# A hybrid decoder layer in fp32 on one core: SwiGLU up-projections by one level of Strassen's algorithm, and a separate down phase

## The chip, the core and the metric

The kernel runs on one core of one Trainium2 chip. The metric is the device time of one execution in microseconds (us); lower is better. TensorE (PE) does matrix products and writes to the accumulators (PSUM), VectorE (DVE), ScalarE (ACT) and GpSimd (POOL) do elementwise work, SyncE (SP) issues the DMAs.

## The reference

One layer: half a SwiGLU feed-forward, a mixing block (sliding-window attention with sinks beside an S5 state-space scan, both gated), and another half feed-forward, over 1024 prompt tokens and 32 sample tokens (1056 columns in the kernel).

```python
D_MODEL = 1024; D_FF = 2816            # 22 tiles of 128

def rms_norm(x, g):
    return x * lax.rsqrt(jnp.mean(x * x, axis=-1, keepdims=True) + 1e-6) * g

def swiglu(x, w1, w3, w2):
    return (jax.nn.silu(x @ w1) * (x @ w3)) @ w2

def trunk_layer(x, ...):
    x = x + 0.5 * swiglu(rms_norm(x, ffn1_norm), ffn1_w1, ffn1_w3, ffn1_w2)
    ...                                  # h = rms_norm(x, mix_norm); proj = h @ w_in; attention; S5
    x = x + merged @ w_out
    x = x + 0.5 * swiglu(rms_norm(x, ffn2_norm), ffn2_w1, ffn2_w3, ffn2_w2)
```

## The kernel before

Features lie on the partitions (8 tiles of 128 for the model width), tokens on the columns: `T` = 1056 in `NC` = 3 chunks of `C` = 352. Every fp32 operand of a large product is split in a high and a low part of 12 bits each (`fp32r`), and a product is three passes: high x high, high x low, low x high (`gemm`, line 153). Weights come from DRAM in units of 8 blocks of 128x128 (`load_w`, line 142): one DMA, a ScalarE copy for the high part, a VectorE subtraction for the low one.

A feed-forward (`ffn`, line 242) goes through 11 groups of two tiles of the inner width. `g1` makes a tile's two up-products (`pa`, `pb`) for the three chunks from x times the norm's weight; `swi` (line 234) multiplies by 1/rms on the result, applies Silu, multiplies and splits. `g2` (line 213) adds the group before, times the rows of `w2`, to x; all inner activations stay in SBUF. The last group runs chunk by chunk, so that `run_last` (line 226) can split x for the next block and sum its squares (`xg_part`, `rstd`) behind it. 1/rms is thus needed only after a product, and the next products start on x itself.

At the start (`first`, line 454), x arrives in pieces of one chunk of one tile, and the first products follow each piece. `hook` (line 442) puts the parameters of the S5 scan beside feed-forward 1: one step of `params_b` in each group from the third on, mostly on GpSimd, with a few TensorE transposes. After the mixing, `merge` makes two tiles of the merged activations at a time, and `g2` adds the group before, times `w_out`, to x.

The order of instructions on each engine comes from the framework's planner, which simulates the program as it is built (`schedule_with_timeline_sim=True`); buffers come from pools with a fixed number of slots: accumulators `mm` and `sm` of four banks each, large tiles `X` (16), `T` (17) and `R` (2).

Of the kernel before, what the change touches and what calls it, by code (L numbers as in the profile page):

```python
# [21 lines left out]
KD = 8  # L22
# [3 lines left out]
NGS = 6         # gate tiles next to the SSM  # L26
# [10 lines left out]
def body(tc, I, O):  # L37
# [4 lines left out]
    with es:  # L42
# [4 lines left out]
        Xp = pool("X", 16)  # L47
        Tp = pool("T", 17)
        Rp = pool("R", 2)
        wr_p = pool("wr", 3)  # L50
        wl_p = pool("wl", 3)
        wh_p = pool("wh", 3)
        gt_p = pool("gt", 3)
        st_p = pool("st", 4)
        sq_p = pool("sq", 4)
        pp_p = pool("pp", 4)
        mm_p = pool("mm", 4, space=PSUM)
        sm_p = pool("sm", 4, space=PSUM)
        dr = pool("dr", 1, space=DRAM)

# [27 lines left out]
        def XT(name, dt=F32R):  # L88
            return big(Xp, "X", name, dt)
# [4 lines left out]
        def RT(name):  # L94
            return big(Rp, "R", name)

        def SQ(name):
            return sq_p.tile([128, C], F32, tag="sq", name=name)
# [4 lines left out]
        def MM(name):  # L103
            return mm_p.tile([128, 512], F32, tag="mm", name=name)[:, :C]

        def SM(name):
            return sm_p.tile([128, 512], F32, tag="sm", name=name)
# [3 lines left out]

        f32 = lambda a: a.bitcast(F32)

# [4 lines left out]
        one = SQ("one")[:, 0:128]  # L118
# [6 lines left out]
        onesh = cst.tile([128, 128], F32R, name="onesh")     # ones where both are of one head  # L125
# [10 lines left out]
        # the tensor engine's clock rises with use: work until the first operands are there  # L136
# [5 lines left out]
        def load_w(src, parts=1, copy=S.copy, lo=V):  # L142
            r = wr_p.tile([128, 8, 128], F32, tag="wr", name="wr")
            l = wl_p.tile([128, 8, 128], F32R, tag="wl", name="wl")
            h = wh_p.tile([128, 8, 128], F32R, tag="wh", name="wh")
            for i in range(parts):
                s = slice(8 // parts * i, 8 // parts * (i + 1))
                dma(r[:, s, :], src[:, s, :])
                copy(h[:, s, :], r[:, s, :])  # L149
                sub(l[:, s, :], r[:, s, :], f32(h[:, s, :]), lo)  # L150
            return h, l

        def gemm(name, c, wks, xs, sm=False):
            """one chunk of one tile of a product: sum over k of w_k^T x_k without the product of the low parts"""
            ps = SM(name)[:, :C] if sm else MM(name)
            n = len(wks)
            for k, (((h, l), kb), (xh, xl)) in enumerate(zip(wks, xs)):
                for i, (w, x) in enumerate(((h, xh), (h, xl), (l, xh))):
                    PE.matmul(ps, w[:, kb, :], x[:, cs(c)], start=k == 0 and i == 0, stop=k == n - 1 and i == 2)  # L159
            return ps  # L160
# [13 lines left out]
        def xg_split(x, g0, xs, k, c):  # L174
            h, l = xs[k]
            g = vec[:, g0 + k:g0 + k + 1]
            act(h[:, cs(c)], x[k][:, cs(c)], AF.Copy, scale=g)
            stt(l[:, cs(c)], x[k][:, cs(c)], g, f32(h[:, cs(c)]), ALU.mult, ALU.subtract)

        def xg_part(x, g0, xs, k, c, acc):  # L180
            xg_split(x, g0, xs, k, c)
            return xg_sq(x, k, c, acc)

        def xg_sq(x, k, c, acc, on_pool=False):
            s = SQ("sq")
            xc = x[k][:, cs(c)]
            if on_pool:
                mul(s, xc, xc, Pl)
            else:
                act(s, xc, AF.Square)  # L190
            if acc is not None:
                add(s, s, acc, Pl)
            return s

        def rstd(r, acc, c):
            ps = SM("ss")
            h, l = (sq_p.tile([128, C], F32R, tag="sq", name="acc" + n) for n in "hl")
            S.copy(h, acc)
            sub(l, acc, f32(h), Pl)
            for i, a in enumerate((h, l)):  # L200
                PE.matmul(ps[:, :C], ones, a, start=i == 0, stop=i == 1)
            y, a = SQ("y"), SQ("a")
            act(y, ps[:, :C], AF.Abs_reciprocal_sqrt, scale=1.0 / 1024, bias=epsx)
            mul(a, y, y)
            stt(a, ps[:, :C], 1024 * EPS, a, ALU.add, ALU.mult)
            ts(a, a, -0.5 / 1024, 1.5, ALU.mult, ALU.add)
            mul(r[:, cs(c)], y, a)
# [3 lines left out]

# [1 line left out]
        def g2(w2, g, hs, x, scale, last):  # L213
            wu = [load_w(w2[2 * g + j]) for j in range(2)]
            order = [(c, m) for c in range(NC) for m in range(KD)] if last else [(c, m) for m in range(KD) for c in range(NC)]
            for c, m in order:
                p = gemm("p2", c, blocks(wu[m // 4], (m % 4 * 2, m % 4 * 2 + 1)), hs)
                o = x[m][:, cs(c)]
                if scale is None:
                    add(o, p, o)  # L220
                else:
                    stt(o, p, scale, o, ALU.mult, ALU.add)
                if last:
                    yield c, m
# [9 lines left out]
        def swi(t, h, l, r, c, pa, pb):  # L234
            tc_ = t[:, cs(c)]
            mul(tc_, pa, r[:, cs(c)])
            act(tc_, tc_, AF.Silu)
            mul(tc_, tc_, r[:, cs(c)])
            mul(tc_, pb(), tc_)
            split(h, l, t, c)  # L240

        def ffn(w1, w3, w2, x, xs, r, hook=None, first=None):
            hs = {}
            ng = NFF // 2

            def g1(g):
                for f in (2 * g, 2 * g + 1):
                    if first and f == 0:
                        hs[f] = first()
                        continue  # L250
                    wa, wb = load_w(w1[f]), load_w(w3[f])
                    t = TT("t")
                    h, l = TT("hh", F32R), TT("hl", F32R)
                    for c in range(NC):
                        swi(t, h, l, r, c, gemm("pa", c, blocks(wa), xs), lambda: gemm("pb", c, blocks(wb), xs))
                    hs[f] = (h, l)

            g1(0)
            for g in range(1, ng):
# [875 lines left out]
```

## Time and profile before

| | us |
|---|---|
| median of 3 runs | 2180.45 (2179.9 to 2182.01) |
| span of the profiled execution | 2178.1 |
| TensorE busy in it | 2156.0 (13545 matmuls) |
| VectorE busy | 1238.8 |
| ScalarE busy | 633.5 |
| GpSimd busy | 390.2 |

The span runs from the first to the last instruction; the remainder of a run lies around it. Busy time of TensorE counts overlapping matmuls, so the distance between their starts tells more than their duration. Feed-forward 1 is the stretch up to about 800 us, the mixing lies between 800 and 1410 us, feed-forward 2 behind that.

### The profile page before, as it was taken

To read this page: it belongs to the slowest core of one execution; us is meant where nothing else is said; L and a number is where in the kernel's file an instruction comes from. 1 tells how busy PE (TensorE), PEld (TensorE's weight loads), DVE (VectorE), ACT (ScalarE), POOL (GpSimd) and SP (SyncE) were. 2 spreads that over 40 slices of the span, in tenths; PEclk is the share of its full clock that TensorE was granted. 3 is DMA by queue.
4 is the path that set the end of the run, shared out by engine and by line. 5 is a ranking of instruction groups with operands and counts; after the bars stand their busy time and mean duration, and the time that the engine had idled before them with its cause. 6 is when DMAs were issued, how large, how long until landed. Compare 5 with 4: busy or idle time off the path is not lost.

```text
span 2178.1 us, 33755 instructions
## 1 busy us (share of the span) xinstructions
PE 2156.0 (99%) x13545; PEld 2132.8 (98%) x13545; DVE 1238.8 (57%) x2357; ACT 633.5 (29%) x1223; POOL 390.2 (18%) x821
## 2 busy tenths in 40 slices
PE   9999999999999999999999999999999999999999
PEld 8999999999999999999998999999999999999999
DVE  9544444454444485758989966854444443444445
ACT  6322222222221152235456631441111111111110
POOL 5342234323430042425101100210000000000000
PEclk9999999999999999999999999999999999999999
DMA  5122112122111135632323571111111111111112
GB/s 184 40 77 63 61 55 72 63 61 65 58 61 59 40 119 197 204 96 75 99 81 114 191 287 47 40 49 49 49 39 41 57 42 45 50 40 49 49 40 80
DMA packets 83133, 173.55 MB, mean 80 GB/s; under 512 B 21200, under 2 KB 46096, under 8 KB 82960
## 3 DMA queue, kind: packets, MB, share of 16 engines
q1 hardware_dynamic: 82976, 171.39, 24.3%
q8 instruction: 106, 1.74, 0.3%
q14 instruction: 51, 0.42, 0.1%
HBM read 132.54 MB, written 35.95 MB: 77 GB/s over the span
## 4 chain that ended last, share of the span: by engine, by line
PE 90%; DVE 5%; ACT 1%; issue 1%; POOL 1%; DMA 1%; SPq 0%; DVEq 0%; ACTq 0%; POOLq 0%
PE p L159 26%; PE pb L159 22%; PE pa L159 22%; PE pj L159 11%; PE pm L159 4%; DVE xl L74 1%; PE pg L159 1%; POOL sq L62 1%; PE sc L766 1%; PE po L807 1%; DVE raw L62 1%; PE pt L792 1%; DVE wl L62 0%; DMA qw<-raw 0%; PE pv L564 0%
## 5 line engine op out<-in xcount | busy, mean ns | idle before, releaser
L74 DVE SCALAR_TENSOR_TENSOR x<-p,x 128x352 f32<-128x352 f32 x528 | 270.2, 522 | 164.8 <-PE p L159 164.2
L149 ACT CAST wh<-wr 128x1024 fp32r<-128x1024 f32 (+1 forms) x176 | 183.9, 1045 | 554.0 <-issue 202.3
L159 PE MATMUL pa<-xh,wh 128*128 128x352 f32 x1056 | 343.6, 325 | 1.4 <-DVE x L62 0.6
L159 PE MATMUL pa<-xl,wh 128*128 128x352 f32 x1056 | 342.3, 324 | 1.7 <-DVE xl L74 1.7
L159 PE MATMUL p<-hh,wh 128*128 128x352 f32 x1056 | 343.2, 325 | 0.3 <-DVE x L74 0.2
L159 PE MATMUL pb<-xh,wh 128*128 128x352 f32 x1056 | 342.4, 324 | 0.0
L159 PE MATMUL pa<-xh,wl 128*128 128x352 f32 x1056 | 342.3, 324 | 0.0
L159 PE MATMUL pb<-xh,wl 128*128 128x352 f32 x1056 | 341.1, 323 | 0.0
L159 PE MATMUL p<-hh,wl 128*128 128x352 f32 x1056 | 340.7, 323 | 0.0
L159 PE MATMUL pb<-xl,wh 128*128 128x352 f32 x1056 | 340.2, 322 | 0.0
L159 PE MATMUL p<-hl,wh 128*128 128x352 f32 x1056 | 340.2, 322 | 0.0
L62 DVE TENSOR_TENSOR wl<-wr,wh 128x1024 fp32r<-128x1024 f32 (+1 forms) x176 | 224.8, 1278 | 70.0 <-ACT wh L149 67.1
L159 PEld LDWEIGHTS pa<-xl,wh 128*128 128x128 f32 x1056 | 199.7, 189 | 4.0 <-DVE xl L74 4.0
L62 DVE TENSOR_TENSOR t<-pa,r 128x352 f32<-128x352 f32 x132 | 69.1, 524 | 233.7 <-PE pa L159 233.5
L159 PEld LDWEIGHTS p<-hh,wh 128*128 128x128 f32 x1056 | 198.5, 188 | 3.5 <-DVE x L74 1.8
L159 PEld LDWEIGHTS pa<-xh,wh 128*128 128x128 f32 x1056 | 199.2, 189 | 2.4 <-DVE x L62 0.9
L62 DVE TENSOR_TENSOR t<-pb,t 128x352 f32<-128x352 f32 x132 | 69.1, 524 | 230.0 <-PE pb L159 229.6
L159 PEld LDWEIGHTS pa<-xh,wl 128*128 128x128 f32 x1056 | 199.5, 189 | 0.2 <-DVE wl L62 0.2
L159 PEld LDWEIGHTS pb<-xl,wh 128*128 128x128 f32 x1056 | 199.1, 189 | 0.0
L159 PEld LDWEIGHTS p<-hl,wh 128*128 128x128 f32 x1056 | 198.8, 188 | 0.0
L159 PEld LDWEIGHTS pb<-xh,wl 128*128 128x128 f32 x1056 | 198.7, 188 | 0.0
L159 PEld LDWEIGHTS p<-hh,wl 128*128 128x128 f32 x1056 | 198.6, 188 | 0.0
(715 smaller groups left out, 3654.1 us busy)
## 6 DMA issues: line engine op xcount, KB each, us to landing
wr<-in_w_in SPq DMA_DIRECT2D x26, 512.0 KB
wr<-in_w2a SPq DMA_DIRECT2D x22, 512.0 KB
wr<-in_w1b SPq DMA_DIRECT2D x22, 512.0 KB
wr<-in_w3b SPq DMA_DIRECT2D x22, 512.0 KB
wr<-in_w2b SPq DMA_DIRECT2D x22, 512.0 KB
wr<-in_w1a SPq DMA_DIRECT2D x21, 512.0 KB
wr<-in_w3a SPq DMA_DIRECT2D x21, 512.0 KB
gd<-gt SPq DMA_DIRECT2D x48, 176.0 KB
```

The lines of the kernel that those rows point to most:

```text
L62: e.tensor_tensor(out=o, in0=a, in1=b, op=op)
L74: V.scalar_tensor_tensor(out=o, in0=a, scalar=s, in1=b, op0=op0, op1=op1)
L149: copy(h[:, s, :], r[:, s, :])
L159: PE.matmul(ps, w[:, kb, :], x[:, cs(c)], start=k == 0 and i == 0, stop=k == n - 1 and i == 2)
L766: PE.matmul(o, st[e_][:, q0:q0 + 128], kk[:, k0:k0 + nk * 128], start=i == 0, stop=i == 1)
L792: PE.transpose(pt[:, kb * 256 + e_ * 128:kb * 256 + e_ * 128 + 128], s_[:, e_, kb * 128:kb * 128 + 128], ident)
L807: PE.matmul(po[:, 0:256], Vs[blk // 4][:, blk % 4, m // 2, :], P[:, a_, kb * 256:kb * 256 + 256], start=i == 0, stop=i == 2 * nk - 1)
```

## The change

Both weight matrices of a tile of the inner width are taken as one matrix of 2 x 2 blocks (w1 and w3 by the two halves of the model width), and x as 2 x 2 blocks (halves of the model width, halves of the columns). One level of Strassen's algorithm makes the four block products from seven, each of 4 k-tiles, with sums of weight blocks (`wprep`) and sums of x blocks (`xprep`, once per feed-forward, kept in SBUF in 28 tiles). Each half of the columns is cut once more into pieces `j` of `J` = 264 columns; `X[op, j]` holds 2 x 264 by (b, j). The seven products accumulate pairwise in the same banks where signs allow (`BANK`, `OPENS`); the rest of the sums is made while they are read out (`up`). Since sums of x blocks must be of the same scale, x is normalized before the products: `sums`, `norm2`, `normalized` at the start, `out_last` and `blocks_of` before feed-forward 2. `up` runs all 22 tiles and writes the inner activations to the DRAM tensor `hid`; then `down` reads them back in groups of 4, 4, 4, 4, 4 and 2 tiles, splits them, and adds the products with `w2` to x, which it reads again from DRAM. `hook` comes after every second tile. The first tile (`first` in `products`) runs six products for the first piece, then six for the second. The output projection runs two groups of two tiles, and the last four tiles in two column pieces. Accumulators are handed over between `pp` (three slots of two banks) with `sm` (two) in `up`, and `mm` with `sm` (four each) elsewhere. Large tiles share one pool of 34 slots, weight units are of 4 blocks (8 slots each), gates use the pool of `sq`.

```diff
+OPS = 4, 3, 1, 2, 5, 7, 6
+OPENS = 4, 3, 1, 6
+BANK = {4: 0, 2: 0, 3: 1, 5: 1, 1: 2, 7: 2, 6: 3}
...
+        def xprep(j, B, X):
+            def put(op, src):
+                h, l = BT(f"X{op}h", F32R), BT(f"X{op}l", F32R)
+                S.copy(h, src)
+                sub(l, src, f32(h))
+                X[op, j] = h, l
+            for op in OPS:
+                if op in XRAW:
+                    put(op, B[XRAW[op]])
+                else:
+                    p, q, f, e = XCOMB[op]
+                    s = wr_p.tile([128, 4, J], F32, tag="wr", name="xs")
+                    f(s, B[p], B[q], e)
+                    put(op, s)
+                yield
+        XRAW = {5: (1, 1), 2: (0, 0)}
+        XCOMB = {3: ((0, 1), (1, 1), sub, V), 4: ((1, 0), (0, 0), sub, Pl), 1: ((0, 0), (1, 1), add, V),
+                 7: ((1, 0), (1, 1), add, Pl), 6: ((0, 0), (0, 1), add, Pl)}
...
+        def wprep(raw):
+            a11, a12, a21, a22 = raw
+            W = {}
+            for op in OPS:
+                if op in RAW:
+                    s = a11 if op == 3 else a22
+                else:
+                    p, q, f, o = {1: (a11, a22, add, None), 5: (a11, a12, add, None), 2: (a21, a22, add, None),
+                                  7: (a12, a22, sub, a12), 6: (a21, a11, sub, a21)}[op]
+                    s = ws_p.tile([128, 4, 128], F32, tag="ws", name="ws") if o is None else o
+                    f(s, p, q)
+                h, l = w4()
+                S.copy(h, s)
+                sub(l, s, f32(h))
+                W[op] = h, l
+            return W
...
+            def one(op, j):
+                b = BANK[op]
+                for k in range(4):
+                    passes(P[b][:, j, 0:J], [t[:, k, :] for t in W[op]], [t[:, k, :] for t in X[op, j]],
+                           k == 0 and op in OPENS, k == 3, skip_group_check=op not in OPENS)
...
+        def up(w1, w3, X, hid, W, hook=None):
...
+                    if op == 4:
+                        S.copy(q, p)
+                    elif op == 3:
+                        S.copy(m3, p)
+                        add(q, q, m3, Pl)
+                    elif op == 1:
+                        S.copy(g, p)
+                        add(g, g, q, Pl)
+                    elif op == 5:
+                        act(a1, p, AF.Silu)
+                        sub(q, q, p)
+                    elif op == 2:
+                        c21 = p_
+                        sub(g, g, p)
+                    elif op == 7:
+                        add(q, q, p)
+                        act(q, q, AF.Silu)
+                        mul(q, q, c21[:, js, :])
+                        dma(hid[f, :, 0:H].rearrange("p (j c) -> p j c", j=2)[:, js, :], q)
+                    else:
+                        add(g, g, p)
+                        mul(g, g, a1, Pl)
+                        dma(hid[f, :, H:T], e2[:, 0:H])
+                if hook:
+                    hook(f)
...
+        def normalized(B, x, g0, a, r):
+            if a:
+                mul(B, B, r.rearrange("p (o c) -> p o c", o=1).to_broadcast([128, 4, J]), Pl)
+            else:
+                for k in range(4):
+                    stt(B[:, k, :], x(k), vec[:, g0 + k:g0 + k + 1], r, ALU.mult, ALU.mult)
+        def norm2(pss):
+            r, y, a = (PP([128, 2, J], n) for n in "rya")
+            for b, ps in enumerate(pss):
+                act(y[:, b], ps, AF.Abs_reciprocal_sqrt, scale=1.0 / 1024, bias=epsx)
+            mul(a, y, y)
+            for b, ps in enumerate(pss):
+                stt(a[:, b], ps, 1024 * EPS, a[:, b], ALU.add, ALU.mult)
+            ts(a, a, -0.5 / 1024, 1.5, ALU.mult, ALU.add)
+            mul(r, y, a)
...
-        it = g2(I["w_out"], 3, (mg.pop(6), mg.pop(7)), x, None, True)
-        xs2 = new_xs()
-        r2 = RT("r2")
-        run_last(it, x, G2, xs2, r2)
+        for acc in out_last(0):
+            pass
+        steps = blocks_of(0, acc)
+        for acc in out_last(1):
+            next(steps, None)
+        for _ in steps:
+            pass
...
+        W0 = wprep(wload(I["w1b"][0], I["w3b"][0]))
+        for _ in blocks_of(1, acc):
+            pass
+        banks(pp=(3, 2), sm=(2, 1))
+        up(I["w1b"], I["w3b"], X, hid, W0)
+        banks(mm=(4, 1), sm=(4, 1))
```

## Rows read from the trace of the kernel before

**Rows 1.** The page, part 1: TensorE's busy time, share of the span, instructions.
```profile
PE 2156.0 (99%) x13545; PEld 2132.8 (98%) x13545; DVE 1238.8 (57%) x2357; ACT 633.5 (29%) x1223; POOL 390.2 (18%) x821
```
**Rows 2.** The page, part 2: busy tenths in 40 slices, and the granted clock.
```profile
DVE  9544444454444485758989966854444443444445
POOL 5342234323430042425101100210000000000000
PEclk9999999999999999999999999999999999999999
```
**Rows 3.** Table by stage: stretch, length, busy (PE PEld DVE ACT POOL), clock, DMA, GB/s.
```profile
0.00:65.00 65.00, 58.70 (x318) 54.31 (x319) 54.99 (x131) 38.84 (x72) 42.44 (x61) 1.00 0.48 162
65.00:775.00 710.00, 710.00 (x4439) 705.87 (x4438) 334.12 (x574) 173.16 (x329) 201.78 (x607) 1.00 0.19 60
775.00:800.00 25.00, 24.08 (x142) 22.46 (x141) 24.70 (x42) 19.77 (x37) 13.42 (x13) 1.00 0.36 131
1400.00:1412.00 12.00, 11.11 (x65) 10.04 (x65) 11.70 (x20) 10.95 (x20) 4.79 (x5) 1.00 0.01 2
1455.00:2140.00 685.00, 685.00 (x4259) 685.00 (x4258) 308.90 (x529) 117.37 (x180) 0.00 (x0) 1.00 0.14 45
```
**Rows 4.** The page, groups of instructions: one of six like groups of up-products.
```profile
L159 PE MATMUL pa<-xh,wh 128*128 128x352 f32 x1056 | 343.6, 325 | 1.4 <-DVE x L62 0.6
```
**Rows 5.** Table by stage, TensorE alone: length, busy (xcount), clock, DMA share, GB/s.
```profile
1450.00:2100.00 650.00, 650.00 (x4042) 1.00 0.15 46
```
**Rows 6.** Timeline of TensorE: start, duration; columns 128, then 256.
```profile
1047.02 0.27 PE L766 MATMUL sc<-kl,qst 128*128 128x128 f32 x1
1047.13 0.34 PE L766 MATMUL sc<-kh,qst 128*128 128x256 f32 x1
...
1101.67 0.28 PE L766 MATMUL sc<-kh,qst 128*128 128x256 f32 x1
1101.79 0.28 PE L766 MATMUL sc<-kl,qst 128*128 128x256 f32 x1
1101.91 0.28 PE L766 MATMUL sc<-kh,qst 128*128 128x256 f32 x1
1102.02 0.28 PE L766 MATMUL sc<-kl,qst 128*128 128x256 f32 x1
```
**Rows 7.** Groups of VectorE by shape: count, busy us, mean ns, idle.
```profile
L62 DVE TENSOR_TENSOR ga<-ga,gs 128x352 f32<-128x352 f32 x24 | 12.4, 519 | 0.1
...
L62 DVE TENSOR_TENSOR raw<-raw,cos 128x1056 f32<-128x1056 f32 x5 | 6.3, 1255 | 9.5 <-DMA qw<-raw 9.5
```
**Rows 8.** Groups of ScalarE by shape.
```profile
L83 ACT ACT_TABLE_LOAD x17 | 21.8, 1283 | 2.4 <-PE py L609 1.4 <-PEq L1104 0.7
...
L83 ACT ACTIVATE gs<-gs 128x1056 f32<-128x1056 f32 x8 | 8.7, 1083 | 1.9 <-DMA gs<-gd 1.9
```
**Rows 9.** GpSimd's operations on one tile: duration ns min/median/max.
```profile
L62 POOL TENSOR_TENSOR qw<-qw,sin x5: 2459/3568/4586, 974.3 to 1043.3; 128x1056 f32<-128x1056 f32 x5
```
**Rows 10.** 5 to 20 us: all engines, then two groups of VectorE there.
```profile
5.00:20.00 15.00, 12.84 (x48) 9.81 (x49) 14.19 (x15) 11.86 (x26) 12.27 (x11) 1.00 1.03 353
...
L74 DVE SCALAR_TENSOR_TENSOR xl<-x,vec,xh 128x352 fp32r<-128x352 f32 x11 | 13.3, 1276 | 0.0
L62 DVE TENSOR_TENSOR wl<-wr,wh 128x512 fp32r<-128x512 f32 x2 | 1.4, 692 | 0.9 <-ACT wh L149 0.9
```
**Rows 11.** The same VectorE operation in 1400 to 1412 us: ns min/median/max.
```profile
L74 DVE SCALAR_TENSOR_TENSOR xl<-x,vec,xh x8: 571/576/1266, 1399.8 to 1411.2; 128x352 fp32r<-128x352 f32 x8
```
**Rows 12.** Table by stage, GpSimd alone, one parameter step; seven more repeat it.
```profile
189.00:205.00 16.00, 5.38 (x15) 1.00 0.20 60
205.00:227.00 22.00, 18.58 (x60) 1.00 0.15 52
227.00:259.00 32.00, 0.00 (x0) 1.00 0.24 70
```
**Rows 13.** Timeline of the start: GpSimd's first use of x, its wait in brackets.
```profile
3.72 0.77 POOL L62 TENSOR_TENSOR sq<-x 128x352 f32<-128x352 f32 x1 [3.28 <-DMA x<-in_x]
```

More of the change, by code (lines that the diff above doesn't have):

```diff
@@ L200, in rstd @@
             for i, a in enumerate((h, l)):
[L201 to L207, printed above, removed]
+                PE.matmul(ps, ones, a, start=i == 0, stop=i == 1)
+        def rstd(r, acc, c):
+            ps = SM("ss")[:, :C]
+            ones_sum(ps, acc)
+            newton(r[:, cs(c)], ps, SQ("y"), SQ("a"))
         def new_xs():
             return [(XT(f"xh{k}"), XT(f"xl{k}")) for k in range(KD)]
[L213 to L224, printed above, removed]
         def run_last(it, x, g0, xs, r):
@@ L231, in run_last @@
                     rstd(r, acc, c)
[L234 to L252, printed above, removed]
-                    h, l = TT("hh", F32R), TT("hl", F32R)
[L254 to L259, printed above, removed]
-                if hook:
-                    hook(g - 1)
-                g1(g)
-                for _ in g2(w2, g - 1, (hs.pop(2 * g - 2), hs.pop(2 * g - 1)), x, 0.5, False):
-                    pass
-            yield from g2(w2, ng - 1, (hs.pop(2 * ng - 2), hs.pop(2 * ng - 1)), x, 0.5, True)
@@ L484, in body @@
+        xp = xprep(0, B[0], X)
+        for _ in range(3):
+            next(xp)
+        ps = [sums(1, B[1], b) for b in range(2)]
+        for _ in xp:
+            pass
+        norm_part(B[1], ps)
+        for _ in xprep(1, B[1], X):
+            pass
+        up(I["w1a"], I["w3a"], X, hid, W0, lambda f: hook(f // 2) if f % 2 else None)
+        banks(mm=(4, 1), sm=(4, 1))
+        x = []
+        it = down(I["w2a"], hid, I["x"], x, GROUPS)
         xsm = new_xs()
-        rm = RT("rm")
+        rm = TT("rm")
@@ L992, in merge, with out_group @@
             mg[m] = (h, l)
+        def out_group(ms):
+            hs = [mg.pop(m) for m in ms]
+            for m in range(KD):
+                wu = load_w(I["w_out"][m][:, ms[0]:ms[-1] + 1])
+                for c in range(NC):
+                    p = gemm("p2", c, blocks(wu, range(len(ms))), hs)
+                    add(x[m][:, cs(c)], p, x[m][:, cs(c)])
         for g in range(4):
@@ new lines, in blocks_of @@
+        def blocks_of(j, acc):
+            B = {(a, b): BT("B") for a in range(2) for b in range(2)}
+            pss = []
+            for b in range(2):
+                pss.append(SM("ss")[:, 0:J])
+                PE.matmul(pss[b], f32(ones), acc[:, b * J:b * J + J], start=True, stop=True)
+                scaled(B[1, b], xj(j, b), G2, 1)
+            r = norm2(pss)
+            for b in range(2):
+                for a in (1, 0):
+                    normalized(B[a, b], xj(j, b), G2, a, r[b])
+            yield
+            yield from xprep(j, B, X)
@@ L1008, in body @@
+        x = []
+        for c, m in down(I["w2b"], hid, xd2, x, GROUPS):
             dma(O["y"][m, :, cs(c)], x[m][:, cs(c)])
+        psum.pop("es").close()
 _OUTS = {
```

298 lines of the change are left out of this document (203 added, 95 removed).

## The prediction

> **What bounds the kernel now.** I read the page first: TensorE is busy for 2156.0 of 2178.1 us [rows 1], and the slices show its clock at full rate throughout [rows 2]. A busy share says little where matmuls are pipelined, so next I looked at the table by stage. In the inner stretches of both feed-forwards (65 to 775 us and 1455 to 2140 us) TensorE and its weight loads never stop, while VectorE works 334 of 710 and 309 of 685 us; at the three edges (start, 775 to 800, 1400 to 1412) VectorE is busy nearly all the time and TensorE has small holes [rows 3]. So the kernel is a queue of matmuls, and a change is worth what it takes from that queue, less what it puts on the edges, where vector work sets the pace.
>
> The price of a place in the queue comes from the distance between starts, not from the mean duration (325 ns, which overlaps the next one). In 650 us of feed-forward 2 there are 4042 matmuls of 352 columns: 160.8 ns each [rows 5]. Matmuls of 256 columns with a fresh 128-column weight load each start 0.12 us apart, and one of 128 columns is followed after 0.11 us [rows 6]. So the distance still shrinks with the columns at 256, and a floor near 0.11 us (the weight load, since 128 columns cost almost what 256 do) lies just below. A straight line from 0.119 (the steps there are 0.12, 0.12 and 0.11) to 0.1608 us gives **122.5 ns at 264 columns**; the ends are 117 (hardly over 256) and 128 (the floor felt).
>
> **The change part by part.**
>
> *Up-projections.* Before, a tile of the inner width takes 2 x 8 x 3 x 3 = 144 matmuls of 352 columns; the six groups of 1056 [rows 4] are 44 such tiles. After, seven products x two column pieces x 4 k x 3 passes = 168 matmuls of 264. Before: 6336 x 0.1608 = 1018.8 us. After: 7392 x 0.1225 = 905.5 us. **Gain 113.3 us** (154 at 117 ns, 73 at 128 ns). This is 20.6 us per tile in place of 23.2.
>
> *Vector work per tile.* Weights: 5 sums and 7 low parts of 128x512 on VectorE at 0.692 us [rows 10] = 8.3 us; seven high parts on ScalarE below 0.7 us each. Out of the accumulators: five VectorE steps of 528 columns, 0.70 us each between 0.519 (352) and 1.255 (1056) [rows 7] = 3.5 us; five on ScalarE, three on GpSimd at about 1.3 us (half of the 2.46 for 1056 [rows 9]). VectorE 11.8 us, GpSimd 4 us under 20.6 us of TensorE: hidden. If that cover fails it costs what VectorE exceeds 20.6 us by. The order of the seven products leaves each accumulator 2 to 3 us between its last read and its next use; I take 0.1 us a tile for misses, **4 us**, bounds 0 and 20.
>
> *Start.* Now the first product needs the finished norm of one column half and sums of it, where before 1/rms was applied to the result. Before 65 us TensorE issued 318 matmuls, 17 of them warm-up: 301 x 0.161 = 48.5 us of work, 16.5 lost [rows 3]. After: 2 x 1.08 MB of x and 1.05 MB of weights at 353 GB/s [rows 10] are 9.1 us behind a first landing near 3.3 us [rows 13], so the half is there at 12 to 13 us; squares, their sums on TensorE, a table load of 1.28 us [rows 8] and two reciprocal roots take it to 16, five short VectorE steps to 19 us. Then GpSimd multiplies two blocks of 128x1056 and subtracts for the first product: 3 x 2.46 to 3.57 us [rows 9], a ScalarE copy of 1.08 [rows 8] and a low part of 1.25: first matmul at 29 to 33 us. In total, from 19 us, GpSimd has 10 such operations (25 to 36 us) and VectorE 18 of 1056, 16 of 264 (about 0.43) and the second norm: 22.6 + 6.9 + 2.8 = 32 us. Side by side and free of each other, tile 0 ends near 53 us. But in 5 to 20 us, with GpSimd busy 12.3 of 15 us, VectorE's operation with two SBUF inputs took 1276 ns [rows 10] where 576 is usual [rows 11], 2.2 times; so stretched, tile 0 ends near 75 us. Lost 32 to 54 us instead of 16.5: net 16 to 38, I take the middle, **27 us**.
>
> The Trainium skill (SBUF — State Buffer, Who interferes with whom) has a rule against this change: a VectorE instruction with two SBUF inputs and a GpSimd instruction that reads SBUF exclude each other for a whole instruction. The trace agrees on the direction but not in full: in those 15 us the undisturbed VectorE work (11 x 0.576 + 2 x 0.69 = 7.7 us) and GpSimd's 12.3 add to 20. By the rule in full the two edges would be dearer; that is the fourth rival below.
>
> *Entry of feed-forward 2.* The last output group runs in two column halves, 384 x 0.1225 = 47.0 us against 288 x 0.1608 = 46.3, and the last merge now stands right before it (three VectorE steps of 0.52 and a ScalarE one, about 2 us, which another group covered before): **2.5 us**. The second half of x is complete only when TensorE has no other work than tile 0's six products on the first half, 8.8 us. Behind it: last square and GpSimd sum (3 us), sums and root with a table load (3), norm (2.8), three GpSimd operations (7.4 to 10.7), copy and low part (2.3): 18.7 to 22 us, so a hole of 10 to 13. VectorE has meanwhile 7 (output adds) + 43 us of preparation from the start of the last half, over 23.5 + 20.6 us of TensorE; stretched as at the start, the hole grows to 28. Before, 65 matmuls in 12 us lost 1.5 [rows 3]. Net 8.5 to 27, I take **17 us**.
>
> *Parameter work beside up.* Each step of the SSM parameters puts GpSimd to work for about 5 and then 19 us of short operations every 70 us [rows 12]; now eight steps come every two tiles, 41 us, 24 + 8 of 41 us. The GpSimd add behind product 3 is due when the next bank is, some 9 us later; a burst of 19 us in front of it costs up to 11 us, eight times, 88 us; nothing if the adds slip between its 60 operations. The order is planned with all of them known, so I take the near end: **10 us**.
>
> *Through DRAM.* 11.9 MB written and read per feed-forward, over DMA engines that are 14 to 19% busy [rows 3], and 22 splits (1.08 ScalarE, 1.25 VectorE) under 46 us groups: hidden. All down matmuls are as many and as wide as before. At each turn from up to down the accumulators change hands, and the first activations and weights were loaded in the last tile: 2 us each, **4 us**; if the first read waited for the last write, its landing, reload and split would make it 8 each.
>
> **Sum.** 113.3 - 27 - 17 - 2.5 - 10 - 4 - 4 = 48.8 us. The profiled execution spans 2178.1 us; the median of the runs is 2180.45, so 2.35 us lie around the span. 2178.1 - 48.8 + 2.35 = **2132 us** (own range 2112 to 2152).
>
> **Rivals.**
> 1. *Cheap edges:* VectorE and GpSimd keep out of each other's way, parameters slip in: 113.3 - 16 - 8.5 - 2.5 - 4 - 4 = 78 us, **2102**. For it: 576 ns in 1400 to 1412 us [rows 11]; against: 1276 ns at the start [rows 10].
> 2. *GpSimd bursts hold the accumulators in feed-forward 1:* five more us in each of eight steps, **2172** (up to 2200). For it: bursts of 18.6 us [rows 12]; against: they are short operations.
> 3. *A bank that comes back late in every tile (the slower side):* product 6 needs an accumulator while that of product 2 is still read by the last multiplication of product 7. If it is given that one, TensorE waits for an add, a Silu and a multiplication, about 2.4 us: 44 x 2.4 = 106, **2238**. The point that decides is 48.8 / 44 = 1.1 us per tile. Against: product 5's accumulator comes free 2 us before.
> 4. *Exclusive port:* VectorE's 32 and GpSimd's 36 us after the first norm add up, tile 0 ends near 90 (26 more than taken), and at the second entry likewise about 30 more: **2190**. Against: the overlap counted above [rows 10].
> 5. *The narrow matmul doesn't scale:* at 130 ns 7392 of them take 961 us, the gain is 58: **2187**; at 137.8 ns the up phase gains nothing. For it: 0.11 at 128 columns; against: 0.12 at 256 [rows 6].
>
> **How the numbers follow.** Forecast 0.56, rivals 0.16, 0.11, 0.07, 0.06 and 0.04 in that order of 1, 2, 4, 3, 5. The range leaves out the better half of rival 1 and the slow rivals 3, 4, 5 with a part of 2: 2095 to 2176. 0.2% (4 us) is about what a measurement of this kernel can tell. Faster: forecast, rival 1 and most of rival 2, 0.82; same 0.04; slower 0.14.
>
> **What would show it.** Distances of 0.1225 us within a product, 20.6 us between like products of neighbouring tiles in feed-forward 2; first product matmul near 30 us, tile 0 ending between 53 and 75; a hole of 10 to 28 us in tile 0 of feed-forward 2, ended by VectorE or GpSimd; holes in tiles 3 to 20 of feed-forward 1 that feed-forward 2 doesn't have would be the parameters. A hole before product 6 in every tile is rival 3. The prediction is wrong if the distance is over 130 ns, or if a hole recurs in every tile.

## The result, and the profile after

The changed kernel is slower: 2278.52 us (2277.34 to 2280.11) against 2180.19 us of the kernel before beside it, a ratio of 1.0451 with a 95% interval of 1.0436 to 1.0465. Forecast were 2132 us and a range up to 2176. The profiled executions span 2278.3 and 2178.1 us: 100.2 us more, where 48.8 us less were predicted.

The page of the changed kernel, parts 1 and 2, to be held against [rows 1, 2]:

```profile
PE 2093.9 (92%) x14757; PEld 2058.5 (90%) x14757; DVE 1424.5 (63%) x2395; ACT 800.3 (35%) x1539; POOL 629.6 (28%) x937
...
PE   5499999999899999999899699965999999999999
...
PEclk7799999999999999999999899987999999999999
```

TensorE has less to do than before (2093.9 against 2156.0 us busy), but the span is longer: its row now has dips at the start, in the middle and at the entry of feed-forward 2, and the clock dips with them. Table by stage (stretch, length, busy PE, PEld, DVE, ACT, POOL, granted clock, DMA share, GB/s), as [rows 3]: start, tile 0, the other up tiles of feed-forward 1, its down phase, mixing, output projection with tile 0 of feed-forward 2, its other up tiles, its down phase:

```profile
0.00:32.00 32.00, 13.62 (x49) 10.76 (x49) 21.59 (x47) 16.31 (x29) 8.69 (x8) 0.85 0.61 212
32.00:108.00 76.00, 35.71 (x199) 33.06 (x200) 63.66 (x108) 34.75 (x56) 47.66 (x58) 0.70 0.10 35
108.00:596.00 488.00, 455.61 (x3624) 447.83 (x3623) 267.85 (x368) 195.98 (x388) 306.96 (x628) 0.97 0.28 93
596.00:865.00 269.00, 259.08 (x1589) 257.65 (x1588) 138.38 (x226) 66.28 (x102) 24.44 (x36) 0.99 0.33 109
865.00:1464.00 599.00, 567.68 (x3626) 550.20 (x3625) 435.53 (x980) 245.60 (x576) 96.60 (x118) 0.97 0.40 130
1464.00:1588.00 124.00, 78.16 (x566) 76.08 (x565) 99.71 (x120) 48.86 (x80) 53.35 (x28) 0.81 0.17 64
1588.00:2016.00 428.00, 428.00 (x3526) 428.00 (x3525) 272.10 (x350) 148.98 (x254) 90.28 (x63) 1.00 0.25 84
2016.00:2278.00 262.00, 256.00 (x1591) 254.94 (x1589) 125.66 (x204) 43.51 (x57) 1.65 (x1) 1.00 0.33 109
```

The seventh line is what the change was priced on: 428 us for 3526 matmuls, 121.4 ns each (122.5 predicted), TensorE never idle, clock 1.00. There a tile takes 20.4 us, where it took 144 x 0.1608 = 23.2. The gain is there. It is overtaken by four other lines.

The stages against the sum of the prediction. Feed-forward 1 is cut at the first projection (796.4 us before, 865.5 after), the mixing at the last product for the merge (1360.0 and 1464.5). The loss at the start is the end of tile 0 (108.6) less its 20.4 us of work, less the 16.5 us lost before; "rest" is what remains of the stretch.

| term, us | predicted | after | last version below |
|---|---|---|---|
| up products, 44 tiles | -113.3 | -121.4 | -121.4 |
| start to the end of tile 0 | +27 | +71.7 | +49 |
| rest of feed-forward 1 (parameters 10, turn 2, misses 2) | +14 | +58.1 | +18 |
| mixing | 0 | +35.4 | +3 |
| rest (output and entry 19.5, turn 2, misses 2) | +23.5 | +56.4 | +41.5 |
| sum | -48.8 | +100.2 | -9.7 |

Every hole of more than 3 us in tile 0 of feed-forward 1, from the timeline of TensorE in 32 to 108 us (start, duration, instruction, idle before and its releaser):

```profile
32.44 0.59 PE L193 MATMUL P<-X4h,wh 128*128 128x264 f32 x1 [13.30 <-ACT X4h L265]
38.45 0.59 PE L193 MATMUL P<-X3h,wh 128*128 128x264 f32 x1 [5.43 <-ACT X3h L265]
...
82.37 0.59 PE L193 MATMUL P<-X2h,wh 128*128 128x264 f32 x1 [27.43 <-ACT e L349]
94.27 0.48 PE L193 MATMUL P<-X3h,wh 128*128 128x264 f32 x1 [4.94 <-DVE e L79]
```

The first product starts at 32.4 us, as predicted (29 to 33). The 27 us before product 2 were not: X2h had long been there. Product 2 adds into the bank of product 4, and that bank waits for ScalarE's copy at line 349. ScalarE in the same stretch:

```profile
68.52 1.07 ACT L265 CAST X4h<-xs 128x1056 fp32r<-128x1056 f32 x1 [11.58 <-POOL xs L79]
73.12 1.07 ACT L265 CAST X3h<-xs 128x1056 fp32r<-128x1056 f32 x1 [3.53 <-DVE xs L79]
...
80.98 1.07 ACT L265 CAST X6h<-xs 128x1056 fp32r<-128x1056 f32 x1
81.95 0.37 ACT L349 COPY e<-P 128x264 f32<-128x264 f32 x1
```

The copy that TensorE waits for stands in ScalarE's queue behind the whole preparation of the second half, which itself waits for GpSimd. And GpSimd slows VectorE. The row of the normalizations (ns min/median/max) has a median of 1.56 us for a shape that takes 0.49 us undisturbed (below), but the 16 are of two kinds: eight take 0.48 to 0.49 us and eight 2.63 to 2.64. One that comes during a GpSimd operation ends some 0.3 us after it, as in the first five operations of both engines:

```profile
L91 DVE SCALAR_TENSOR_TENSOR B<-B,vec,r x16: 479/1562/2640, 22.6 to 71.3; 128x264 f32<-128x264 f32 x16
...
22.59 0.49 DVE L91 SCALAR_TENSOR_TENSOR B<-B,vec,r 128x264 f32<-128x264 f32 x1
22.69 2.66 POOL L79 TENSOR_TENSOR B<-B,r 128x1056 f32<-128x1056 f32 x1 [22.24 <-DMA B<-in_xb]
23.00 2.64 DVE L91 SCALAR_TENSOR_TENSOR B<-B,vec,r 128x264 f32<-128x264 f32 x1
25.32 2.60 POOL L79 TENSOR_TENSOR B<-B,r 128x1056 f32<-128x1056 f32 x1
25.57 2.64 DVE L91 SCALAR_TENSOR_TENSOR B<-B,vec,r 128x264 f32<-128x264 f32 x1
```

In the other tiles of feed-forward 1 (the starts of neighbouring tiles lie 20.6 to 27.6 us apart, 26 to 28 in about every third) the recurring hole is this one: product 6 waits for a VectorE readout step, that for a GpSimd sum, and that stands among parameter operations. The operand of the first sum (line 351) was there at 297.6 us; GpSimd came to it at 305.2, after 14 parameter operations placed ahead of it (timelines of TensorE, VectorE, ScalarE and GpSimd):

```profile
312.82 0.53 PE L193 MATMUL P<-X6h,wh 128*128 128x264 f32 x1 [4.21 <-DVE e L79]
...
308.70 0.70 DVE L79 TENSOR_TENSOR e<-e,P 128x528 f32<-128x528 f32 x1 [5.99 <-POOL e L79]
...
297.04 0.60 ACT L351 COPY e<-P 128x528 f32<-128x528 f32 x1
...
304.75 0.48 POOL L79 TENSOR_TENSOR tm<-bb,pwr 128x128 f32<-128x128 f32 x1
305.19 1.36 POOL L79 TENSOR_TENSOR e<-e 128x528 f32<-128x528 f32 x1
306.47 0.92 POOL L79 TENSOR_TENSOR ba<-tm 128x128 f32<-128x128 f32 x2
307.32 1.34 POOL L79 TENSOR_TENSOR e<-e,e 128x528 f32<-128x528 f32 x1
```

The entry of feed-forward 2 repeats the start: in order, an output add on VectorE behind eight normalizations, four sums of squares on GpSimd (9.14 us for the four; one at 1496.7 us took 1.33), the accumulators' change of hands behind the second norm, and once more the copy at line 349 behind the casts:

```profile
1512.76 0.59 PE L193 MATMUL p<-mh,wh 128*128 128x264 f32 x1 [9.07 <-DVE x L79]
...
1533.35 2.13 PE L1204 MATMUL ss<-sq,ones 128*128 128x264 f32 x4 [9.35 <-POOL sq L79]
...
1544.25 0.56 PE L193 MATMUL P<-X4h,wh 128*128 128x264 f32 x1 [8.78 <-DVE a L91]
...
1567.81 0.59 PE L193 MATMUL P<-X2h,wh 128*128 128x264 f32 x1 [17.03 <-ACT e L349]
```

The 35 us in the mixing had no term at all, and no single wait in the trace explains them.

### The profile page after: what moved, and what is told of

Same layout as the page of the kernel before. It is cut to its first block, busy times and chain, and to the rows that moved or that the text cites. A ratio compares the mean times of both kernels' runs of the same rounds, so it can differ in the third digit from the quotient of the medians.

```text
span 2278.3 us, 37882 instructions
## 1 busy us (share of the span) xinstructions
PE 2093.9 (92%) x14757; PEld 2058.5 (90%) x14757; DVE 1424.5 (63%) x2395; ACT 800.3 (35%) x1539; POOL 629.6 (28%) x937
## 4 chain that ended last, share of the span: by engine, by line
PE 64%; DVE 8%; POOL 7%; DMA 3%; issue 2%; ACT 1%; SPq 1%; POOLq 0%; ACTq 0%; DVEq 0%
PE p L193 25%; PE P L193 20%; PE pj L193 12%; PE pm L193 4%; POOL tm L79 4%; POOL e L79 1%; DVE B L91 1%; SPq L563 1%; DVE wl L79 1%; PE pg L193 1%; DVE raw L79 1%; DMA pa_d<-mt 0%; DMA hr<-hid 0%; PE pt L962 0%; PE po L977 0%
## 5 line engine op out<-in xcount | busy, mean ns | idle before, releaser
L79 DVE TENSOR_TENSOR wl<-wr,wh 128x512 fp32r<-128x512 f32 (+1 forms) x360 | 250.2, 695 | 128.6 <-ACT wh L303 94.3
L91 DVE SCALAR_TENSOR_TENSOR x<-p,x 128x352 f32<-128x352 f32 x288 | 150.0, 523 | 242.6 <-PE p L193 235.6
L181 ACT CAST wh<-wr 128x512 fp32r<-128x512 f32 (+1 forms) x184 | 110.5, 601 | 451.2 <-PE p L193 322.8
L79 DVE TENSOR_TENSOR e<-e,P 128x528 f32<-128x528 f32 (+1 forms) x228 | 154.9, 682 | 135.5 <-PE P L193 75.8
L79 POOL TENSOR_TENSOR e<-e 128x528 f32<-128x528 f32 (+1 forms) x90 | 130.0, 1445 | 370.5 <-DVE e L79 238.2
L193 PE MATMUL pj<-xh,wh 128*128 128x352 f32 x624 | 205.7, 330 | 3.9 <-DVE gt L79 3.6
L193 PE MATMUL pj<-xl,wh 128*128 128x352 f32 x624 | 204.4, 328 | 0.0
L193 PE MATMUL pj<-xh,wl 128*128 128x352 f32 x624 | 204.1, 327 | 0.0
L79 DVE TENSOR_TENSOR ws<-wr 128x512 f32<-128x512 f32 x132 | 146.1, 1109 | 10.9 <-DMA wr<-in_w1a 6.8
L193 PE MATMUL P<-X2h,wh 128*128 128x264 f32 x352 | 101.3, 288 | 44.5 <-ACT e L349 44.5
L193 PEld LDWEIGHTS pj<-xh,wh 128*128 128x128 f32 x624 | 119.3, 191 | 5.2 <-DVE gt L79 4.0
```

The costliest lines, as they stand in the source:

```text
L79: e.tensor_tensor(out=o, in0=a, in1=b, op=op)
L91: V.scalar_tensor_tensor(out=o, in0=a, scalar=s, in1=b, op0=op0, op1=op1)
L181: S.copy(h[:, 0:m, :], r[:, i:i + m, :])
L193: PE.matmul(ps, a, b, start=first and i == 0, stop=last and i == 2, **kw)
```

## The experiments

Theory: the loss is not in the products but in the order of short work on the other engines (queue order at the entries, GpSimd beside VectorE, GpSimd between accumulator and readout) and, in the mixing, in the buffers. Main rival: the added preparation is simply too much vector work, and no order helps. A time given without an interval is that of one execution.

**Readout ahead of the second half's preparation.** The preparation becomes a generator of which one step runs after each readout of the first piece; in feed-forward 2 the accumulators change hands before it.

```diff
+                    if prep and f == 0 and js.start == 0 and js.stop == 1:
+                        if op == 7:
+                            for _ in prep:
+                                pass
+                        else:
+                            next(prep)
...
-        norm_part(B[1], ps)
-        for _ in xprep(1, B[1], X):
-            pass
```

> Only the order changes: the preparation of the second half of the columns (normalization, the sums of blocks of X, their casts) is interleaved with the first tile of each FFN, so that each product's readout stands ahead of the next preparation step in ScalarE's queue, instead of behind all of them; and FFN2 changes its accumulator pools before the second half's last step. Theory QUEUE (the changed kernel's 27.4 and 17.3 us holes in the first tiles are a readout copy standing behind casts): both holes shrink to a few us and the time falls by 27 to 44 us, to 2235 to 2251 us. Rival PREPARATION (the casts and sums themselves are what the products wait for, so whatever is put first makes the other late): the first tiles keep 70 or more and 40 or more us, time 2265 to 2280 us.

2274.8 us, 4 less, hardly more than the runs of one kernel differ by. The hole before product 2 went from 27.4 to 2.3 us, but one of 10.9 before product 7 and others took its place, 12.4 us of them before transposes of the parameter work that the planner now put into tile 0, and tile 0 took 77.3 us after 76.2. The rival's side: in 60 to 90 us VectorE was busy for 29.85 of 30 us, mostly with the preparation, though part of that was waiting behind GpSimd, which was busy for 28.4. But the edit was also only half of one: with one step between two readouts, ScalarE's queue holds a cast that waits for the normalization ahead of the next readout.

**Preparation on VectorE alone.** Normalization and the three sums of blocks that ran on GpSimd move to VectorE; ScalarE's scaling of GpSimd's half falls away with it.

```diff
-        XCOMB = {3: ((0, 1), (1, 1), sub, V), 4: ((1, 0), (0, 0), sub, Pl), 1: ((0, 0), (1, 1), add, V),
-                 7: ((1, 0), (1, 1), add, Pl), 6: ((0, 0), (0, 1), add, Pl)}
+        XCOMB = {3: ((0, 1), (1, 1), sub, V), 4: ((1, 0), (0, 0), sub, V), 1: ((0, 0), (1, 1), add, V),
+                 7: ((1, 0), (1, 1), add, V), 6: ((0, 0), (0, 1), add, V)}
...
-            if a:
-                mul(B, B, r.rearrange("p (o c) -> p o c", o=1).to_broadcast([128, 4, J]), Pl)
-            else:
-                for k in range(4):
-                    stt(B[:, k, :], x(k), vec[:, g0 + k:g0 + k + 1], r, ALU.mult, ALU.mult)
+            for k in range(4):
+                stt(B[:, k, :], x(4 * a + k), vec[:, g0 + 4 * a + k:g0 + 4 * a + k + 1], r, ALU.mult, ALU.mult)
...
```

> Only the engine changes: the normalization of the first pieces and the sums of blocks of X run on VectorE alone, none on GpSimd. Theory PORT (the 8 VectorE operations of 128x264 took 11.94 us, 1.49 us each, because GpSimd worked on the same SBUF at the time): the same form falls to about 0.43 us each, the first tile shortens and the time falls by 15 to 35 us, to 2243 to 2263 us. Rival LATENCY (these operations are slow for another reason): they still take over 1.2 us each, and VectorE now has more to do, so the time is 2278 to 2295 us.

2262.2 us, 16 less. The same form, now 32 of them:

```profile
L91 DVE SCALAR_TENSOR_TENSOR B<-B,vec,r x32: 482/488/678, 20.9 to 57.3; 128x264 f32<-128x264 f32 x32
```

GpSimd's share came over to VectorE, and VectorE needs 13.9 us for 32 normalizations where it needed 23.9 for 16. Tile 0 hardly moved (75.1 us), since the copies still stood behind the casts.

**Readout sums on VectorE.**

```diff
-                        add(q, q, m3, Pl)
+                        add(q, q, m3)
...
-                        add(g, g, q, Pl)
+                        add(g, g, q)
...
-                        mul(g, g, a1, Pl)
+                        mul(g, g, a1)
```

> Only the engine changes: the three readout operations of an up tile that ran on GpSimd (two sums and the gating product) run on VectorE. Theory BURST (in the first FFN every third tile waits some 4 us for a readout sum that stands behind a step of parameter work on GpSimd, and the clock then falls for several us): the tiles of FFN1 go from 27 and 21 to 20.4 to 21.5 us each, 45 to 55 us in all, time 2223 to 2235 us. Rival STEP (the parameter step takes the time by its own TensorE, ScalarE or VectorE work): every third tile still takes 24 us or more, time 2265 us or more.

2233.1 us, 45 less. Tiles 1 to 21 of feed-forward 1 take 449.5 us in place of 487.6, with the parameter work still beside them: 20.4 to 21.9 us each but for two late ones of 26. The whole "rest of feed-forward 1" of the table falls from 58.1 to 13.5 us (first projection at 823.7, end of tile 0 at 111.4 us). The three operations of some 1.4 us were worth what they held, not what they cost.

**All three.**

> The three edits before together: readout ahead of the second half's preparation, normalization and block sums on VectorE, readout sums on VectorE. If the three theories hold and their gains add up: 2278 - 27 to 44 - 15 to 35 - 45 to 55, but the start's parts overlap, so 2160 to 2190 us, about level with the kernel before. If one of the three causes is another's cover: 2200 us or more.

2222.0 us, ratio 1.0187 (1.017 to 1.0204), 57 less than the changed kernel, less than the 65 of the three alone. Tile 0 still takes 72.3 us: ScalarE waits 11.61 us on a cast for the second half, with the readout of product 1 (line 354) behind it:

```profile
59.87 1.07 ACT L265 CAST X4h<-xs 128x1056 fp32r<-128x1056 f32 x1 [11.61 <-DVE xs L79]
60.85 0.37 ACT L354 COPY e<-P 128x264 f32<-128x264 f32 x1
```

A second hole in it, 9.3 and 1.7 us, is again before transposes of the parameter work, which GpSimd had not made ready.

**The mixing: buffer pools, in the kernel before.** The diff gives all large tiles one pool of 34 slots (16 + 17 + 2 before) and the gates the pool of `sq` (5 in place of 4 + 3). Both poolings, in the kernel before and with nothing else of the change:

```diff
-        Xp = pool("X", 16)
-        Tp = pool("T", 17)
-        Rp = pool("R", 2)
+        Tp = pool("T", 34)
...
-        gt_p = pool("gt", 3)
...
-        sq_p = pool("sq", 4)
+        sq_p = pool("sq", 5)
...
```

> The kernel before with the buffer pools of the changed kernel and nothing else: one pool of 34 large tiles in place of three of 16, 17 and 2, and the gates' buffers in the pool of sq (5 slots in place of 4 and 3). Theory POOLS (the 35 us that the changed kernel loses in the mixing come from the shared pools): the mixing, 564.6 us from the first projection to the last gated product, becomes about 600 us and the time about 2215 us. Rival ORDER (they come from the planner's other order or from other weight units): 2180 us, within 3.

2225.2 us, 44.5 us more, 29.8 of them in the mixing (593.4 us from first projection to last merge product, to the tenth what it took with all three edits above) and 12.3 before the first projection. Then each pooling by itself:

> The kernel before with the three pools of large tiles (16, 17, 2) made one of 34, the gates' buffers left in a pool of their own. The run with both poolings lost 28.8 us in the mixing and 12 us up to the end of feed-forward 1. If the large tiles' pool is the cause: mixing about 593 us, time 2215 to 2225 us. If the gates' pool is: 2180 us, within 4, here.

> The kernel before with the gates' buffers in the pool of sq (5 slots in place of 4 and 3), the pools of large tiles as before. If the gates' pool is the cause of the loss in the mixing (a gate's product is read out late, because its buffer is held by another's DMA): mixing about 593 us, time 2210 to 2225 us. If the large tiles' pool is: 2180 us, within 4, here.

2220.7 and 2208.4 us: both cost, 26.2 and 21.9 us of it in the mixing, and the two don't add up. Much of the loss lies at the tile `z` of the SSM's output: the gate products `pg` behind its cast fill TensorE while the last attention units finish. From the kernel before, with both poolings, and from the changed kernel (first and last start):

```profile
L878 ACT CAST zh<-zr x4: 2023/2036/2089, 1163.1 to 1177.3; 128x1024 fp32r<-128x1024 f32 x4
```
```profile
L875 ACT CAST zh<-zr x4: 1947/2017/2060, 1220.0 to 1233.1; 128x1024 fp32r<-128x1024 f32 x4
```
```profile
L1048 ACT CAST zh<-zr x4: 1944/2005/2073, 1280.7 to 1293.7; 128x1024 fp32r<-128x1024 f32 x4
```

Counted from the first projection (796.4, 808.7, 865.5 us), `z` is cast at 367, 411 and 415 us, while the last product of an attention unit starts at 453, 446 and 450. So little is left to put between the products of those units. TensorE alone in the 75 us from 375 us on (stretch, length, busy, granted clock, DMA share, GB/s), in the kernel before, with both poolings, in the changed kernel, and in that with the pools apart (next run):

```profile
1171.40:1246.40 75.00, 70.87 (x462) 0.98 0.40 142
...
1183.70:1258.70 75.00, 57.80 (x342) 0.89 0.33 118
...
1240.50:1315.50 75.00, 57.24 (x338) 0.89 0.29 96
...
1240.10:1315.10 75.00, 69.94 (x447) 0.95 0.31 118
```

With the gates' pool alone `z` is cast at 387 us, so its delay is not all of the loss there. Which slot the planner waited for is not in a trace; with the large pool alone the four loads of `z` were issued at 1186.8 us and the first cast started at 1213.6, with other work ordered before it.

**The changed kernel with the pools apart.** Pools of 16, 16 and 2 with the blocks of X, `e` and the down phase's tiles placed in them, gates apart, and two buffers in place of three for sums of weights:

```diff
-                h, l = BT(f"X{op}h", F32R), BT(f"X{op}l", F32R)
+                h, l = (BT(f"X{op}{n}", F32R, "T" if j else "X") for n in "hl")
...
-                e1, e2 = TT("e1"), TT("e2")
+                e1, e2 = ((TT, RT, XT)[f % 3](n, F32) for n in ("e1", "e2"))
```

> The changed kernel with the buffer pools of the kernel before in their parts: large tiles in three pools of 16, 16 and 2, with the blocks of X and x placed in them by hand, and the gates' buffers apart from sq (paid for with one buffer less for sums of weights). Theory POOLS: the casts of z and the glu products move ahead of the attention's end again, the mixing goes from 599 to 565 to 575 us and the time to 2240 to 2255 us. Rival: with other work around it the mixing finds another late buffer and stays at 590 us or more, time 2270 us or more.

2247.8 us, 31 less: the mixing takes 567 us, and `z` is cast 369 us after the first projection. The first projection itself stays at 865 us.

**Pools, vector preparation, vector sums, and the preparation behind all six readouts.**

> The run before with, in addition, normalization, block sums and readout sums on VectorE, and the whole preparation of the second half put behind the readouts of the first piece's six products (the earlier order put its first steps between them, where ScalarE waited 11.6 us for a normalization ahead of a readout). From 2222 us of the earlier combination: pools 24 to 29 less; the order 5 to 20 less if the readouts were the wait, 0 if the preparation's own work on VectorE (some 23 us a half) is. So 2173 to 2198 us, 2190 being what the pools alone give.

2177.4 us. Tile 0 went from 72.3 to 66.8 us. What held it now, beside 13.5 us before the second half's first product, was a TensorE transpose of the parameter work, placed by the planner in tile 0, 8.8 us ahead of its operand from GpSimd.

**Parameter work later.** `e` is a readout of tile 5, so that nothing of the parameters can start before it.

```diff
...
-            pexp(dt_, ldt, q1, q2)
+            stt(th, e[:, 0:16], 0.0, ldt, ALU.mult, ALU.add)
+            pexp(dt_, th, q1, q2)
```

> The run before (2177.4 us) with one thing more: the S5 parameter work starts after tile 5 in place of tile 3, and its first operation also reads a readout of tile 5 times zero, so that it can't be pulled ahead into tile 0. In the run before, TensorE's queue stood 9.1 us in tile 0 before a transpose of a parameter tile that GpSimd hadn't made yet, and VectorE did some 4 to 5 us of parameter operations between the first half's and the second half's preparation. If that is what keeps tile 0 at 66.8 us: tile 0 falls to 50 to 57 us and the time to 2160 to 2168 us. If the second half's preparation on VectorE alone keeps it: tile 0 stays over 60 us, and the time is 2172 us or more. The parameter steps themselves move two tiles later, and may then hold the last tiles of FFN1 for up to 10 us, as the last two did before.

2199.3 us, ratio 1.0084 (1.0067 to 1.0101): 22 us worse, though tile 0 did fall to 55.4 us. Each step, due every two tiles, now held TensorE for some 5 us, and its tile took 25 to 28 us. The tile `ba`, which GpSimd makes for the transposes:

```profile
L82 POOL TENSOR_TENSOR ba<-tm x28: 456/460/478, 225.1 to 519.9; 128x128 f32<-128x128 f32 x28
...
  PEld ptr L536: 27.8, 16
...
  PE ptr L536: 24.5, 13
```

TensorE and its loads waited 13 and 16 times on it. My reading: started at tile 0, GpSimd has a lead over the transposes; started at tile 5 with a step due every two tiles, it has none.

**Parameter work spread.** The work starts on a readout of tile 1; the steps stand after tiles 3, 6, ... 21 and one in the down phase.

> As the run before, but the parameter work starts on a readout of tile 1, its eight steps stand after every third tile (3, 6, ... 21) and the last one in the down phase, in place of after every second tile from 7 on, where each step held TensorE's queue for 5 to 6 us before its transposes (tiles of 26 us beside tiles of 20.4). Theory LEAD (GpSimd needs about three tiles for a step; a step that is due sooner makes TensorE wait): tile 0 stays at 55 us, the others go to 20.4 to 21.1 us, FFN1's up phase from 543.7 to 495 us, time 2148 to 2160 us. Rival PLACE (a step's transposes wait 5 us wherever they stand): tiles with a step stay at 26 us, 7 of them, time 2180 to 2192 us.

**2169.8 us, ratio 0.9951 (0.9934 to 0.9967)**: faster than both kernels, than the kernel before by half a per cent. Tiles 6 to 21 take 20.4 to 21.1 us; TensorE and its loads wait 3 and 5 times on `ba`, 5.9 and 6.9 us. The first two steps still cost 3.4 to 5.8 us. Whether the earlier start or the wider spacing did it was not separated. The time is 10 us over the upper end of what was expected: from the run before, the stretch between the last product of up and the first projection grew from 260.9 to 271.8 us, with a parameter step now in it. Its table by stage, same cuts as above:

```profile
0.00:30.00 30.00, 14.18 (x49) 10.79 (x49) 18.93 (x42) 12.93 (x21) 0.20 (x4) 0.89 0.65 226
30.00:86.00 56.00, 37.74 (x202) 34.12 (x203) 48.68 (x71) 28.26 (x43) 0.00 (x0) 0.76 0.14 46
86.00:531.00 445.00, 439.13 (x3613) 435.01 (x3611) 301.22 (x496) 188.09 (x373) 219.53 (x504) 1.00 0.30 103
531.00:802.00 271.00, 261.26 (x1597) 258.61 (x1597) 137.30 (x228) 72.19 (x120) 55.39 (x139) 0.99 0.32 107
802.00:1369.00 567.00, 555.00 (x3627) 543.40 (x3626) 435.20 (x982) 245.55 (x579) 103.62 (x120) 0.99 0.41 138
1369.00:1477.00 108.00, 80.86 (x564) 78.09 (x564) 87.73 (x143) 41.85 (x63) 19.79 (x14) 0.84 0.19 71
...
```

**The preparation back on GpSimd, in that version.**

> The run before (2169.8 us, tile 0 at 55.2 us) with normalization of half the blocks and three of the five sums of X back on GpSimd, as in the changed kernel; nothing else differs. Theory PORT: VectorE's 128x264 normalizations take about 1.5 us each again beside GpSimd's work (0.49 us alone), so that work given to GpSimd is no relief: tile 0 takes 62 to 75 us and the time is 2180 to 2195 us, both feed-forwards' entries taken together. Rival RELIEF: with readouts and parameters out of its way, GpSimd takes some 13 us of work off VectorE's chain: tile 0 at 45 to 53 us, time 2155 to 2168 us.

2196.5 us, 26.7 us more, some 23 of them at the two entries: tile 0 takes 64.2 us after 55.2 in feed-forward 1 and 56.2 after 46.3 in feed-forward 2, and both begin later. With nothing else in the way, the two engines side by side are slower than VectorE alone. The normalizations in this run and in the one before:

```profile
L94 DVE SCALAR_TENSOR_TENSOR B<-B,vec,r x16: 480/1562/2644, 22.5 to 71.5; 128x264 f32<-128x264 f32 x16
```
```profile
L94 DVE SCALAR_TENSOR_TENSOR B<-B,vec,r x32: 481/486/494, 21.8 to 60.0; 128x264 f32<-128x264 f32 x32
```

## Why the prediction was wrong

- **Up products.** Right: 121.4 ns and 20.4 us a tile against 122.5 and 20.6 predicted, no hole that recurs in the tiles of feed-forward 2. Rivals 3 (a bank late in every tile) and 5 (a narrow matmul that doesn't scale) fall with it. Vector work under a tile was hidden, as predicted; the 4 us of misses were not there. Neither of the two signs of being wrong that the prediction named came; both looked at the products, and the loss was elsewhere.
- **Mixing.** The largest omission of mechanism: the front matter lists the merged pools, and the prediction gave them no term, neither a cost nor a cover. They cost 29.8 us of it in the kernel before, and apart they gave back 32 of the 35 in the changed one. A part of the change that is priced at nothing needs a reason, and this one had none.
- **Start.** Mis-sized, 71.7 for 27. The first product came when predicted; the end of tile 0 did not (108.6 us, bounds 53 to 75). Three things failed. The work was counted as if each engine could take it in the best order; the planner put readouts behind casts. The work itself was short: the count from 19 us on gave VectorE 32 us beside GpSimd's 25 to 36, leaving out the weights of tiles 0 and 1 and the readouts. In the last version, with order, parameters and GpSimd out of the way, VectorE is busy for 59.5 us between 19 and 86 us (some 15 of them GpSimd's former share), and tile 0 ends at 86: VectorE is close to the bound there, and even so the term is 49 us, above its upper bound of 38. So the main rival holds for that part. And the clock had no term: in 32 to 108 us TensorE is busy for 35.7 us with 163 matmuls of products (19.8 us at 121.4 ns), 32 sums of squares (7.3 us) and four transposes, so some 8 us went to the lower clock, in the last version some 10 (estimates from these rows); before, the clock was 1.00 there [rows 3].
- **Parameter work.** Wrong end taken: 10 us out of 0 to 88. The rest of feed-forward 1 cost 58.1 us for 14, and moving the three readout sums alone brought it to 13.5. Rival 2's mechanism, with a chance of 0.11, was what happened, at about its middle price: its parameters at 50 us (10 and five more in each of eight steps), measured 54 without turn and misses. The argument against it ("they are short operations", "the order is planned with all of them known") was the error: operations of 0.5 us are short, but the sum was placed behind 14 of them and came 6 us late for VectorE, and each hole of over 3 us in these tiles is followed by a stretch at a lower granted clock.
- **Readings.** The 75 us at the upper end of the start has no sum: VectorE's 32 us stretched 2.2 times from 19 us on end at 89, stretched only while GpSimd's 36 us last, at 71. The 3.28 us of [rows 13] is the wait before the first use of x; the use is at 3.7 us, which changes nothing.
- **Entry of feed-forward 2.** 56.4 us for 23.5. A hole of 10 to 28 us was predicted and 17 us are there before product 2, but there are three more of about 9 us, two of them from GpSimd and VectorE queues that the sum treated as free (output adds behind normalizations, sums of squares behind block sums); the third, the change of accumulators behind the second norm, had no term.
- **Exclusive port** (rival 4). Its mechanism is shown: a normalization takes 2.64 us when it meets a GpSimd operation and 0.49 when it doesn't, and the run that put the preparation back on GpSimd lost 26.7 us, most of it over both entries. By the Trainium skill (SBUF — State Buffer, Who interferes with whom) a VectorE instruction with two SBUF inputs and a GpSimd instruction that reads SBUF exclude each other. The trace of the changed kernel agrees: from 22.6 us on each of four GpSimd operations of 2.54 to 2.66 us holds one normalization to its end, and four more slip in between at 0.49. The eight take 11.9 us, less than the sum of 3.9 and GpSimd's 10.3 us, since neighbours overlap by some 0.3 us. A GpSimd operation that makes four normalizations, some 2 us of work on VectorE, takes some 2 us from VectorE (2.64 less 0.49): nothing is gained. I had read the 2.2 times of [rows 10], a mean, as a middle case and gave the rule 0.07.
- **Where the terms add.** Start, parameters and entry were bounded each by itself, and the range was made from single misses. They missed together, which I put down to one kind of cause: the change puts short work on three in-order queues, and where one stands, TensorE stands. The 48.8 us of forecast gain could carry one such miss, not three and the pools.

What stays open: which slots make the planner order `z` late; whether the entries can be brought under VectorE's 60 us by giving ScalarE a part; the 17 us that the last version loses between up and the mixing beyond the down products. Some 11 of them came with the parameter step in that stretch, and a hole of 5.4 us ends at 573.3 us behind a late read of `hid`; the rest was not followed.

## What to carry to other kernels

A saving in the matmul queue is worth what is left after the edges, so count the vector work up to the first full tile engine by engine, in queue order, with weights and readouts in it. Buffer pools are part of the schedule: a change that merges them changes what the planner can run ahead in stages whose code it doesn't touch, and needs a term of its own. An operation that stands between an accumulator and its reuse belongs on an engine with no background work, however short the operation is.

## What the runs showed of the hardware

- Work moved from VectorE to GpSimd can lengthen VectorE's own time: 32 normalizations on VectorE alone took 13.2 to 13.9 us, 16 of them beside GpSimd 23.9 us. Of these 16, eight took 0.49 us and eight 2.64; each long one ended some 0.3 us after a GpSimd operation of some 2.6 us that it had met. The median of 1.56 us hides that.
- Holes cost twice. The granted clock, 1.00 over the 428 us without a hole, was 0.70 on the mean over tile 0 of the changed kernel and 0.81 over the entry of feed-forward 2, between the lower level (1.2 GHz) and the full one (2.4 GHz); matmuls right behind a long hole took 0.59 us where 0.285 is usual. Around the 4.2 us hole at 309 us it was 0.91 over 12 us and 0.96 over the 15 us behind.
